# Hymba layer, Up stage: when the weight operands of the next block are made, where the taps stand, and when the weights are fetched

## The chip, the cores and the metric

The kernel runs on one core of one Trainium2 chip. The metric is the device time of one execution in microseconds (us). The median of three runs before the change is 1077.51 us (1074.84 to 1078.73).

## What is computed

One decoder layer on x (1024 x 1024, float32): attention and retention in a mixer, then a feed-forward part. The change lies in the feed-forward part, of which the reference says:

```python
h = rms_norm(x, ffn_pre_norm[l])
u = causal_depthwise_conv(jnp.einsum('bsd,df->bsf', h, w_up[l]), conv_w[l], conv_b[l])
u_gate, u_val = jnp.split(u, 2, axis=-1)
y = jax.nn.gelu(u_gate, approximate=True) * u_val
y = jnp.einsum('bsf,fd->bsd', y, w_down[l])
x = x + rms_norm(y, ffn_post_norm[l])
```

with D_MODEL 1024, D_FF 2816 (22 blocks of 128 for the gate and 22 for the value) and a convolution of three taps.

## The kernel before, in words

The Up product is done in 22 blocks. A block i holds 128 columns of the gate and 128 of the value, and its four quarters (gate and value by the two halves of the sequence) come out of a Strassen-Winograd scheme of seven products, named by their weight operand: B11, T1, T2, B21, T3, T4 and B22. A product (`prod`) is 4 x 3 matmuls of 128x128 by 128x512: each float32 operand is split into a high and a low float32r part, and `mm3` adds high*high, low*high and high*low. For blocks 0 to 10 (early blocks, `EARLY = 11`) the products B11 and B21 have been made in an earlier stage and lie in DRAM (`ud`), so they need five products here; blocks 11 to 21 (late blocks) need all seven. The order is 11, 0, 12, 1, ..., 21, 10, so a pair of blocks is 12 products, 144 matmuls.

In PSUM a block has the accumulator PA (in a row: B11 or, in an early block, the stored part and T2; then T2, T3 and T4 are added), PC (T1, then B22 added) and, if late, PB (B21). PA is copied out between the products that are added to it: `h` after the first (L796), `u` after T2 (L808, late blocks only) and after T3 (L814), `uv` after T4 (L819), all on ACT. DVE adds: `ug` low half from PB and h (L811), `uv` high half from PC and u (L815), `ug` high half from PC (L821). The first product of the next block (`head`) is issued between T3 and T4 of the running one.

The weights of a block come by two transfers of 512 KB (L721: a11 and a12 in the first, a21 and a22 in the second) into a tile `raw`. Of the pool's eight slots six hold activations in this stage, so two `raw` tiles live at once, and the next fetch waits until the last split of the older one has been read out. DVE makes combinations of the quarters (L732, L733, L735, L743), and each operand is split: the high part on ACT (L114 in `oh`, or L712 in `sh`), the low part on DVE (L115, L713). `sh` has four slots and `oh` five, so a split also waits for the product that used its slot.

The gate of a block (`gate`, `taps`) is the convolution: for value and gate ACT makes the first tap (L701), DVE adds two more (L704); then GELU on ACT (L829), the product on DVE (L830) and a store to DRAM (`yd`, 512 KB). SP issues all these transfers in order on one queue. The Down stage (matmuls pd, steps of 24 matmuls) loads yd and w_d, combines and splits them in the same way (`feed`, L848, L115, L713).

The program is written block by block: `prep(then)` fetches and makes all operands of the next block, `strassen(i, then)` issues the products, `gate` the convolution. That is not the order in which the engines get them: a scheduler sorts the instructions by its own model of their times and of free slots, except where `in_turn` ties them to the written order. On each engine the sorted instructions are then run strictly one after the other.

Of the kernel before, what the change touches and what calls it, by code (L numbers as in the profile page):

```python
# [11 lines left out]
ALU = mybir.AluOpType  # L12
# [15 lines left out]
def tile_hymba_layer(  # L28
# [29 lines left out]
    def small(name):  # L58
        return pss.tile([P, H], F32, tag="psm", name=name)
# [99 lines left out]
    def ttile(name, dt=F32):  # L159
        return m.tile([P, H], dt, tag="t", name=name, bufs=5)  # L160
# [507 lines left out]
    for hh in range(2):  # L668
# [5 lines left out]
        if hh == 0:  # L674
# [25 lines left out]
    def taps(a, u, b, c0, n=H):  # L700
        nc.scalar.activation(a, u[:, c0 : c0 + n], AF.Identity, scale=cvp[:, b, 2:3], bias=cvp[:, b, 3:4])  # L701
        for d, tap in ((1, 1), (2, 0)):
            s = max(0, d - c0)
            nc.vector.scalar_tensor_tensor(  # L704
                out=a[:, s:], in0=u[:, c0 + s - d : c0 + n - d], scalar=cvp[:, b, tap : tap + 1], in1=a[:, s:],
                op0=ALU.mult, op1=ALU.add,
            )

    def ssplit(src, name):
        hi = ftile(0, f"sh_{name}", F32R)  # L710
        lo = ftile(1, f"sl_{name}", F32R)
        in_turn("sh", nc.scalar.activation(hi, src, AF.Copy))  # L712
        nc.vector.tensor_tensor(out=lo, in0=src, in1=hi.bitcast(F32), op=ALU.subtract)  # L713
        return hi, lo

    ops = {}

    def prep(i):
        raw = ttile(f"raw{i}", F32)
        for t in range(2):  # L720
            nc.sync.dma_start(raw[:, 2 * t : 2 * t + 2, :], w_u[t * NF + i].rearrange("p (a b) -> p a b", a=2))  # L721
        a11, a12, a21, a22 = [raw[:, c, :] for c in range(4)]
        o = {}
        ug[i] = gtile(f"ug{i}")
        if i < EARLY:
            seeds[i] = ftile(2, f"p1_{i}")
            nc.sync.dma_start(seeds[i], ud[i, :, 0:H])
            nc.sync.dma_start(ug[i][:, 0:H], ud[i, :, H:D])
        else:
            o["B11"] = split(a11, f"u{i}a11")  # L730
        s3, s1 = a11, a21
        nc.vector.tensor_tensor(out=s3, in0=a11, in1=a21, op=ALU.subtract)  # L732
        nc.vector.tensor_tensor(out=s1, in0=a21, in1=a22, op=ALU.add)  # L733
        s2 = xtile(f"s2_{i}")
        nc.vector.tensor_tensor(out=s2, in0=a22, in1=s3, op=ALU.subtract)  # L735
        if i < EARLY:
            o["T2"] = ssplit(s2, f"u{i}s2")
            o["T1"] = ssplit(s1, f"u{i}s1")
        else:
            o["T1"] = ssplit(s1, f"u{i}s1")  # L740
            o["T2"] = ssplit(s2, f"u{i}s2")
            o["B21"] = split(a12, f"u{i}a12")
        nc.vector.tensor_tensor(out=s2, in0=a12, in1=s2, op=ALU.subtract)  # L743
        o["T3"] = ssplit(s3, f"u{i}s3")
        o["T4"] = split(a22, f"u{i}a22")
        o["B22"] = ssplit(s2, f"u{i}s4")
        ops[i] = o
# [17 lines left out]
    ug, seeds, heads = {}, {}, {}  # L765

    def early_load(i):
        raw = load_w(w_u[i], 1024, f"e{i}")
# [19 lines left out]
    def head(i):  # L788
        ps = big(f"PA_{i}")
        u = ftile(2, f"h{i}")  # L790
        if i < EARLY:
            nc.scalar.activation(ps, seeds.pop(i), AF.Copy)
            prod(i, "T2", ps, first=False)
        else:
            prod(i, "B11", ps)
        nc.scalar.activation(u, ps, AF.Copy)  # L796
        heads[i] = ps, u

    def strassen(i, then):
        pa, u = heads.pop(i)  # L800
        g, v = ug.pop(i), vtile(f"uv{i}")
        pc = small(f"PC_{i}")
        prod(i, "T1", pc)
        u2 = u
        if i >= EARLY:
            prod(i, "T2", pa, first=False)
            u2 = ftile(2, f"u2_{i}")
            nc.scalar.activation(u2, pa, AF.Copy)  # L808
            pb = (small, big)[i % 2](f"PB_{i}")
            prod(i, "B21", pb)  # L810
            nc.vector.tensor_tensor(out=g[:, lo], in0=pb, in1=u, op=ALU.add)  # L811
# [12 lines left out]
    def gate(i, g, v):
        a = []
        for t, u in enumerate((v, g)):
            a.append(wtile(f"a{t}_{i}"))
            taps(a[t], u, (1 - t) * NF + i, 0, D)
        nc.scalar.activation(a[1], a[1], AF.Gelu_apprx_tanh)  # L829
        nc.vector.tensor_tensor(out=a[1], in0=a[0], in1=a[1], op=ALU.mult)  # L830
        nc.sync.dma_start(yd[i], a[1])
# [219 lines left out]
    prep(order[0])  # L1051
    head(order[0])
    for i, then in zip(order, order[1:] + [None]):
        if then is not None:
            prep(then)
        else:
# [99 lines left out]
```

## Time and profile before

| | |
|---|---|
| median of three runs | 1077.51 us (1074.84 to 1078.73) |
| the profiled execution's own time | 1077.63 us |
| its span, first to last instruction | 1075.6 us |
| share of the span busy: PE / DVE / ACT / POOL | 98% / 77% / 55% / 10% |
| the Up stage: first weight load of a head to the first wait of Down | 481.6 to 855.5 us |
| mean granted TensorE clock | 0.997 |

A PE row "busy" hides waits, since matmuls overlap: one takes 389 ns but they start every 0.23 us. The waits are therefore read from the weight loads (PEld), one of which stands ahead of each matmul. In timelines the bracket at the end of a row gives the idle time of that engine just before and what ended it.

### The profile page before, as it was taken

To read this page: it belongs to the slowest core of one execution; us is meant where nothing else is said; L and a number is where in the kernel's file an instruction comes from. 1 tells how busy PE (TensorE), PEld (TensorE's weight loads), DVE (VectorE), ACT (ScalarE), POOL (GpSimd) and SP (SyncE) were. 2 spreads that over 40 slices of the span, in tenths; PEclk is the share of its full clock that TensorE was granted. 3 is DMA by queue.
4 is the path that set the end of the run, shared out by engine and by line. 5 is a ranking of instruction groups with operands and counts; after the bars stand their busy time and mean duration, and the time that the engine had idled before them with its cause. 6 is when DMAs were issued, how large, how long until landed. Compare 5 with 4: busy or idle time off the path is not lost.

```text
span 1075.6 us, 14268 instructions
## 1 busy us (share of the span) xinstructions
PE 1051.2 (98%) x5004; PEld 886.6 (82%) x5004; DVE 829.6 (77%) x1428; ACT 587.2 (55%) x1140; POOL 103.9 (10%) x123
## 2 busy tenths in 40 slices
PE   8999999999999999999999999999999999999995
PEld 6988998988988888888887787787878788888884
DVE  5567768668676686987796887968789998859687
ACT  6556763467643567664555455544555545444461
POOL 1013232124322210000000000000000000000011
PEclk9999999999999999999999999999999999999998
DMA  8421551221231473763323323232233784625663
GB/s 287 138 79 59 177 167 51 80 83 55 78 101 57 169 242 125 267 229 124 137 98 118 118 79 137 92 124 91 106 131 115 263 301 140 225 98 189 231 194 129
DMA packets 54727, 152.81 MB, mean 142 GB/s; under 512 B 6400, under 2 KB 6528, under 8 KB 54656
## 3 DMA queue, kind: packets, MB, share of 16 engines
q1 hardware_dynamic: 53504, 149.81, 40.7%
q10 hardware_dynamic: 1152, 2.10, 0.5%
q8 instruction: 39, 0.64, 0.2%
q14 instruction: 32, 0.26, 0.1%
HBM read 126.20 MB, written 25.69 MB: 141 GB/s over the span
## 4 chain that ended last, share of the span: by engine, by line
PE 63%; DVE 17%; DMA 9%; issue 6%; ACT 4%; POOL 1%; SPq 0%; DVEq 0%; POOLq 0%; ACTq 0%
DMA raw<-w_u 6%; DVE a L704 6%; PE pd L123 5%; PE pd L124 5%; PE pd L125 5%; PE ps_r L123 3%; PE ps_r L125 3%; PE ps_r L124 3%; PE po L123 3%; PE po L125 3%; PE po L124 3%; PE pn L123 2%; PE pn L124 2%; PE pn L125 2%; PE PA L123 2%
## 5 line engine op out<-in xcount | busy, mean ns | idle before, releaser
L123 PE MATMUL pd<-oh_d,sh_d 128*128 128x512 f32 x264 | 102.8, 389 | 1.0 <-DVE ug L821 1.0
L124 PE MATMUL pd<-ol_d,sh_d 128*128 128x512 f32 x264 | 102.7, 389 | 0.0
L125 PE MATMUL pd<-oh_d,sl_d 128*128 128x512 f32 x264 | 102.7, 389 | 0.0
L973 POOL TENSOR_TENSOR fs<-fs,mhalf 128x1 f32<-128x1 f32 x8 | 5.8, 730 | 623.6 <-DVE fs L972 623.6
L123 PE MATMUL pn<-oh_n,xh 128*128 128x384 f32 x192 | 65.8, 343 | 0.2 <-DVE gp L285 0.2
L125 PE MATMUL pn<-oh_n,xl 128*128 128x384 f32 x192 | 64.5, 336 | 0.0
L124 PE MATMUL pn<-ol_n,xh 128*128 128x384 f32 x192 | 64.3, 335 | 0.0
L704 DVE SCALAR_TENSOR_TENSOR a<-uv,cvp,a 128x1023 f32<-128x1023 f32 (+1 forms) x44 | 56.2, 1277 | 9.5 <-ACT a L701 9.5
L123 PEld LDWEIGHTS pd<-oh_d,sh_d 128*128 128x128 f32 x264 | 49.5, 188 | 11.7 <-DVE ug L821 1.4
L125 PEld LDWEIGHTS pd<-oh_d,sl_d 128*128 128x128 f32 x264 | 49.5, 188 | 10.3
L124 PEld LDWEIGHTS pd<-ol_d,sh_d 128*128 128x128 f32 x264 | 49.6, 188 | 10.2
L704 DVE SCALAR_TENSOR_TENSOR a<-ug,cvp,a 128x1023 f32<-128x1023 f32 (+1 forms) x44 | 56.2, 1277 | 0.5 <-ACT a L701 0.5
L123 PE MATMUL ps_r<-xh,oh_r 128*128 128x512 f32 x128 | 50.7, 396 | 0.0
L125 PE MATMUL ps_r<-xh,ol_r 128*128 128x512 f32 x128 | 50.0, 390 | 0.0
L124 PE MATMUL ps_r<-xl,oh_r 128*128 128x512 f32 x128 | 49.9, 390 | 0.0
L701 ACT ACTIVATE a<-ug,cvp 128x1024 f32<-128x1024 f32 x22 | 27.4, 1246 | 38.0 <-DVE ug L821 35.7
L331 ACT ACTIVATE s<-s,sc,r 128x128 f32<-128x128 f32 x64 | 31.0, 487 | 29.6 <-DVE sc L325 29.6
L732 DVE TENSOR_TENSOR raw<-raw 128x512 f32<-128x512 f32 x22 | 15.2, 689 | 37.5 <-DMA raw<-w_u 37.5
L829 ACT ACTIVATE a<-a 128x1024 f32<-128x1024 f32 x22 | 23.4, 1062 | 36.2 <-DVE a L704 36.2
L712 ACT ACTIVATE sh_d<-r 128x512 fp32r<-128x512 f32 x33 | 20.9, 632 | 39.5 <-PE pd L124 22.2
L114 ACT ACTIVATE oh_o<-wr_o 128x512 fp32r<-128x512 f32 x32 | 19.9, 634 | 36.8 <-PE po L125 35.6
L114 ACT ACTIVATE oh_n<-wr_n 128x384 fp32r<-128x384 f32 x48 | 24.3, 523 | 28.7 <-PE ps_q L124 10.3
(1177 smaller groups left out, 3293.8 us busy)
## 6 DMA issues: line engine op xcount, KB each, us to landing
raw<-w_u SPq DMA_DIRECT2D x44, 512.0 KB, 4.5
yd<-a SPq DMA_DIRECT2D x22, 512.0 KB, 3.3
r<-yd SPq DMA_DIRECT2D x22, 512.0 KB, 5.8
wr_n<-w_inN SPq DMA_DIRECT2D x24, 384.0 KB, 3.0
wr_r<-w_inT SPq DMA_DIRECT2D x16, 512.0 KB, 3.3
wr_o<-w_o SPq DMA_DIRECT2D x16, 512.0 KB, 3.5
wr_e<-w_u SPq DMA_DIRECT2D x11, 512.0 KB, 4.7
ud<-e SPq DMA_DIRECT2D x11, 512.0 KB, 3.9
```

Of the source, the lines that this page charges most:

```text
L114: in_turn("oh", nc.scalar.activation(hi[:, :n], src, AF.Copy))
L123: ins = nc.tensor.matmul(ps, lh, rh, start=first, stop=False, skip_group_check=onto)
L124: nc.tensor.matmul(ps, lh, rl, start=False, stop=False, skip_group_check=onto)
L125: nc.tensor.matmul(ps, ll, rh, start=False, stop=end, skip_group_check=onto)
L331: nc.scalar.activation(s[:, i, :], s[:, i, :], AF.Exp, scale=r8, bias=c[:, 1, i : i + 1], accum_out=c[:, 3, i : i + 1])
L701: nc.scalar.activation(a, u[:, c0 : c0 + n], AF.Identity, scale=cvp[:, b, 2:3], bias=cvp[:, b, 3:4])
L704: nc.vector.scalar_tensor_tensor(out=a[:, s:], in0=u[:, c0 + s - d : c0 + n - d], scalar=cvp[:, b, tap : tap + 1], in1=a[:, s:], op0=ALU.m ...
L712: in_turn("sh", nc.scalar.activation(hi, src, AF.Copy))
L732: nc.vector.tensor_tensor(out=s3, in0=a11, in1=a21, op=ALU.subtract)
L829: nc.scalar.activation(a[1], a[1], AF.Gelu_apprx_tanh)
L973: nc.gpsimd.tensor_tensor(out=ss[:, 2:3], in0=ss[:, 3:4], in1=mhalf[:, 0:1], op=ALU.pow)
```

## The change

`prep` is cut into `fetch` (the two transfers, and the stored part of an early block), `fetch_g` (the tile ug and its stored half), `combos` (B11's split if late, then three combinations) and `part` (the split of one named operand). `body` replaces `strassen` and `gate`: it issues the products of block i and, at written places between them, `make` for the operands of the next block. The convolution of the block before is written in two halves inside the running block (`gate_v` value, `gate_g` gate, GELU, product and store). `fetch` is called for the block after the next at the start of a block. In early blocks T1 is issued after T3. The last gate is written behind the splits of the first two Down steps.

```diff
-    def prep(i):
-        raw = ttile(f"raw{i}", F32)
+    def fetch(i):
+        raw = raws[i] = ttile(f"raw{i}", F32)
         for t in range(2):
             nc.sync.dma_start(raw[:, 2 * t : 2 * t + 2, :], w_u[t * NF + i].rearrange("p (a b) -> p a b", a=2))
+        if i < EARLY:
+            seeds[i] = ftile(3, f"p1_{i}")
+            nc.sync.dma_start(seeds[i], ud[i, :, 0:H])
+        ops[i] = {}
+
+    def fetch_g(i):
         ug[i] = gtile(f"ug{i}")
         if i < EARLY:
-            seeds[i] = ftile(2, f"p1_{i}")
-            nc.sync.dma_start(seeds[i], ud[i, :, 0:H])
             nc.sync.dma_start(ug[i][:, 0:H], ud[i, :, H:D])
...
+    def combos(i):
+        if i >= EARLY:
+            part(i, "B11")
+        raw = raws[i]
+        a11, a12, a21, a22 = [raw[:, c, :] for c in range(4)]
+        s2 = s4s[i] = xtile(f"s2_{i}")
+        nc.vector.tensor_tensor(out=a11, in0=a11, in1=a21, op=ALU.subtract)
+        nc.vector.tensor_tensor(out=s2, in0=a22, in1=a11, op=ALU.subtract)
+        nc.vector.tensor_tensor(out=a21, in0=a21, in1=a22, op=ALU.add)
+
+    def part(i, *names):
+        raw = raws[i]
+        for x in names:
+            if x == "B22":
+                nc.vector.tensor_tensor(out=s4s[i], in0=raw[:, 1, :], in1=s4s[i], op=ALU.subtract)
...
-    def strassen(i, then):
+    def body(i, then, before):
+        def make(*names):
+            if then is not None:
+                part(then, *names)
+
         pa, u = heads.pop(i)
-        g, v = ug.pop(i), vtile(f"uv{i}")
-        pc = small(f"PC_{i}")
-        prod(i, "T1", pc)
-        u2 = u
-        if i >= EARLY:
+        g, pc = ug.pop(i), small(f"PC_{i}")
+        full = i >= EARLY
+        if then is not None:
+            combos(then)
+        if full:
+            prod(i, "T1", pc)
+            make("T2")
+            if before:
+                gate_v(*before)
             prod(i, "T2", pa, first=False)
             u2 = ftile(2, f"u2_{i}")
             nc.scalar.activation(u2, pa, AF.Copy)
+            make("T3")
             pb = (small, big)[i % 2](f"PB_{i}")
             prod(i, "B21", pb)
+            if before:
+                gate_g()
+            if then is not None:
+                fetch_g(then)
             nc.vector.tensor_tensor(out=g[:, lo], in0=pb, in1=u, op=ALU.add)
+        else:
+            gate_v(*before)
+        v = vtile(f"uv{i}")
         prod(i, "T3", pa, first=False)
-        u3 = ftile(2, f"u3_{i}")
+        u3 = ftile(3, f"u3_{i}")
         nc.scalar.activation(u3, pa, AF.Copy)
+        if not full:
+            u2 = u
+            prod(i, "T1", pc)
         nc.vector.tensor_tensor(out=v[:, hi], in0=pc, in1=u3, op=ALU.add)
+        make("T1")
+        if not full:
+            gate_g()
+            if then is not None:
+                fetch_g(then)
         if then is not None:
             head(then)
+        if not full:
+            make("T2", "T3", "B21")
+        make("T4")
         prod(i, "T4", pa, first=False)
         nc.scalar.activation(v[:, lo], pa, AF.Copy)
+        if then is None:
+            feed(0)
         prod(i, "B22", pc, first=False)
         nc.vector.tensor_tensor(out=g[:, hi], in0=pc, in1=u2, op=ALU.add)
-        return g, v
...
+        make("B22")
+        return i, g, v
...
+    for k, i in enumerate(order):
+        if k + 2 < len(order):
+            fetch(order[k + 2])
+        if k + 1 == len(order):
             for t in range(AHEAD_LOAD):
                 load(t)
-            feed(0)
-        gate(i, *strassen(i, then))
-    ready = 1
+        before = body(i, order[k + 1] if k + 1 < len(order) else None, before)
+    feed(1)
+    gate_v(*before)
+    gate_g()
+    ready = 2
```

The scheduler decides what this makes of each engine's order. Three places in the middle of the stage show it (late blocks 18 and 19, early blocks 6, 7 and 8).

ACT, from the copy of block 18's head to its copy after T2 (oh_u19 are the splits of block 19's B11 and B21, `a` the convolution's tiles of block 6, sh_u18 the last split of block 18, sh_u7 splits of block 7). Before:

```order
L796 ACTIVATE h_6857<-PA_6856 128x512
L114 ACTIVATE oh_u19a_7054<-raw_7050 128x512
L819 ACTIVATE uv_6827<-PA_6737 128x512
L792 ACTIVATE PA_6997<-p_7_6912 128x512
L701 ACTIVATE a_6_6897<-uv_6827,cvp 128x1024
L114 ACTIVATE oh_u19a_7070<-raw_7050 128x512
L712 ACTIVATE sh_u18s_6823<-s_18_6800 128x512
L701 ACTIVATE a_6_6901<-ug_6651,cvp 128x1024
L712 ACTIVATE sh_u7s_6919<-s_7_6917 128x512
L712 ACTIVATE sh_u7s_6923<-raw_6908 128x512
L808 ACTIVATE u_18_6966<-PA_6856 128x512
```

and now:

```order
L797 ACTIVATE h_6841<-PA_6840 128x512
L862 ACTIVATE uv_6800<-PA_6731 128x512
L701 ACTIVATE a_6_6926<-uv_6800,cvp 128x1024
L712 ACTIVATE sh_u18B_6898<-s_18_6792 128x512
L114 ACTIVATE oh_u19B_7048<-raw_6902 128x512
L114 ACTIVATE oh_u19B_7123<-raw_6902 128x512
L701 ACTIVATE a_6_6961<-ug_6708,cvp 128x1024
L712 ACTIVATE sh_u7T_6922<-s_7_6906 128x512
L712 ACTIVATE sh_u7T_6944<-raw_6782 128x512
L832 ACTIVATE u_18_6942<-PA_6840 128x512
```

The first split of block 19 stood second, ahead of the copy `uv` and both first taps of block 6; it now stands behind `uv`, the value's tap and the last split of block 18, and the splits of B11 and B21 are neighbours.

DVE, in the early block 7, from the first combination of block 8's weights (raw_7168 before, raw_7042 now) to the `uv` add. Before (12 rows from the combination on):

```order
L732 TENSOR_TENSOR raw_7168<-raw_7168 128x512
L733 TENSOR_TENSOR raw_7168<-raw_7168 128x512
L704 SCALAR_TENSOR_TENSOR a_18_7039<-uv_6940,cvp,a_18_7039 128x1023
L821 TENSOR_TENSOR ug_6793<-PC_6941,u_18_6966 128x512
L704 SCALAR_TENSOR_TENSOR a_18_7039<-uv_6940,cvp,a_18_7039 128x1022
L713 TENSOR_TENSOR sl_u19s_7063<-raw_7050,sh_u19s_7062 128x512
L704 SCALAR_TENSOR_TENSOR a_18_7043<-ug_6793,cvp,a_18_7043 128x1023
L713 TENSOR_TENSOR sl_u19s_7067<-s_19_7060,sh_u19s_7066 128x512
L704 SCALAR_TENSOR_TENSOR a_18_7043<-ug_6793,cvp,a_18_7043 128x1022
L743 TENSOR_TENSOR s_19_7060<-raw_7050,s_19_7060 128x512
L713 TENSOR_TENSOR sl_u19s_7076<-raw_7050,sh_u19s_7075 128x512
L815 TENSOR_TENSOR uv_7087<-PC_7088,u_7_7113 128x512
```

and now (from the second combination on; the first stands just ahead of it, as before):

```order
L739 TENSOR_TENSOR s_8_7166<-raw_7042 128x512
L704 SCALAR_TENSOR_TENSOR a_18_7056<-uv_6971,cvp,a_18_7056 128x1023
L866 TENSOR_TENSOR ug_6839<-PC_6905,u_18_6942 128x512
L704 SCALAR_TENSOR_TENSOR a_18_7056<-uv_6971,cvp,a_18_7056 128x1022
L713 TENSOR_TENSOR sl_u19T_7089<-raw_6902,sh_u19T_7088 128x512
L704 SCALAR_TENSOR_TENSOR a_18_7092<-ug_6839,cvp,a_18_7092 128x1023
L713 TENSOR_TENSOR sl_u19T_7116<-s_19_7052,sh_u19T_7115 128x512
L704 SCALAR_TENSOR_TENSOR a_18_7092<-ug_6839,cvp,a_18_7092 128x1022
L850 TENSOR_TENSOR uv_7060<-PC_7047,u_7_7073 128x512
L713 TENSOR_TENSOR sl_u19T_7120<-raw_6902,sh_u19T_7119 128x512
L812 TENSOR_TENSOR a_18_7092<-a_18_7056,a_18_7092 128x1024
L746 TENSOR_TENSOR s_19_7052<-raw_6902,s_19_7052 128x512
```

The first combination of block 8 has kept its place; the `uv` add has moved ahead of two operations, and the last operation that reads the weights of block 19 (s_19, L746) has moved from ahead of the split of T3 to behind the product `a` (L812).

SP, the same stretch: stores `yd`, weight fetches `raw`, stored parts p and ug. Before:

```order
L831 DMA yd<-a_6_6901 128x1024
L721 DMA raw_7168<-w_u 128x1024 x2
L728 DMA ug_7171<-ud 128x512
L721 DMA raw_7310<-w_u 128x1024
L727 DMA p_8_7172<-ud 128x512
L831 DMA yd<-a_18_7043 128x1024
L721 DMA raw_7310<-w_u 128x1024
L831 DMA yd<-a_7_7161 128x1024
```

and now:

```order
L813 DMA yd<-a_6_6961 128x1024
L724 DMA p_8_7045<-ud 128x512
L721 DMA raw_7042<-w_u 128x1024 x2
L730 DMA ug_7228<-ud 128x512
L813 DMA yd<-a_18_7092 128x1024
L721 DMA raw_7162<-w_u 128x1024 x2
L813 DMA yd<-a_7_7221 128x1024
```

The two halves of a late block's weights (raw_7310, now raw_7162) were issued one before and one behind the store of block 18; now both stand behind it.

## Rows read from the trace of the kernel before

**Rows 1.** The page, part 1: busy us (share of the span) xinstructions.

```profile
PE 1051.2 (98%) x5004; PEld 886.6 (82%) x5004; DVE 829.6 (77%) x1428; ACT 587.2 (55%) x1140; POOL 103.9 (10%) x123
```

**Rows 2.** Windows by engine: busy (x instructions); then granted clock, DMA share, GB/s.

```profile
470.00:482.00 12.00, 12.00 (x54) 9.85 (x53) 8.90 (x16) 5.50 (x11) 0.00 (x0) 1.00 0.94 336
...
584.00:822.00 238.00, 231.66 (x1009) 188.27 (x1009) 193.07 (x248) 125.48 (x185) 0.00 (x0) 1.00 0.31 109
822.00:856.00 34.00, 31.93 (x138) 25.22 (x137) 30.13 (x40) 17.81 (x26) 0.00 (x0) 1.00 0.71 242
856.00:880.00 24.00, 24.00 (x108) 19.85 (x107) 23.49 (x36) 12.08 (x20) 0.00 (x0) 1.00 0.63 234
```

**Rows 3.** Waits of the weight loads, 480 to 862: us in total, times, longest.

```profile
PEld PA L123 <- ACT u L808: 8.7, 7, 2.7
PEld PC L123 <- DVE uv L815: 2.7, 5, 1.0
PEld PA L123 <- ACT u L814: 1.8, 2, 1.4
PEld pd L123 <- DVE ug L821: 1.4, 1, 1.4
```

**Rows 4.** The tile PA: weight loads of two heads; the range is of their starts.

```profile
L123 PEld LDWEIGHTS PA<-hh,oh_u11a x4: 187/188/188, 481.6 to 483.6; 128*128 128x128 f32 x4
...
L123 PEld LDWEIGHTS PA<-T2h,sh_u0s x4: 188/188/188, 495.2 to 497.2; 128*128 128x128 f32 x4
```

**Rows 5.** Timeline of the weight loads: start, us, operation, idle before it.

```profile
591.51 0.19 PEld L123 LDWEIGHTS PA<-T3h,sh_u14s 128*128 128x128 f32 x1 [1.14 <-ACT u L808]
...
855.54 0.19 PEld L123 LDWEIGHTS pd<-oh_d,sh_d 128*128 128x128 f32 x1 [1.38 <-DVE ug L821]
```

**Rows 6.** Timeline of DVE, one early block, 604 to 614.5.

```profile
604.27 0.69 DVE L732 TENSOR_TENSOR raw<-raw 128x512 f32<-128x512 f32 x1 [3.61 <-DMA raw<-w_u]
...
605.61 1.28 DVE L704 SCALAR_TENSOR_TENSOR a<-uv,cvp,a 128x1023 f32<-128x1023 f32 x1
606.80 0.68 DVE L821 TENSOR_TENSOR ug<-PC,u 128x512 f32<-128x512 f32 x1
607.40 1.27 DVE L704 SCALAR_TENSOR_TENSOR a<-uv,cvp,a 128x1022 f32<-128x1022 f32 x1
...
613.99 1.21 DVE L830 TENSOR_TENSOR a<-a,a 128x1024 f32<-128x1024 f32 x1
```

**Rows 7.** Timeline of SP: when the weight fetches were issued.

```profile
578.47 0.33 SPq L721 DMA_DIRECT2D raw<-w_u  x1
...
598.89 1.00 SPq L721 DMA_DIRECT2D raw<-w_u  x2
...
613.50 0.33 SPq L721 DMA_DIRECT2D raw<-w_u  x1
...
615.23 0.33 SPq L831 DMA_DIRECT2D yd<-a  x1
...
632.93 0.81 SPq L721 DMA_DIRECT2D raw<-w_u  x2
...
782.91 0.33 SPq L721 DMA_DIRECT2D raw<-w_u  x1
```

**Rows 8.** Timeline of ACT: splits that wait for weights, and what follows.

```profile
583.37 0.63 ACT L114 ACTIVATE oh_u15a<-raw 128x512 fp32r<-128x512 f32 x1 [4.49 <-DMA raw<-w_u]
...
588.69 1.25 ACT L701 ACTIVATE a<-ug,cvp 128x1024 f32<-128x1024 f32 x1 [1.51 <-DVE ug L821]
...
617.42 0.63 ACT L114 ACTIVATE oh_u16a<-raw 128x512 fp32r<-128x512 f32 x1 [3.51 <-DMA raw<-w_u]
...
787.51 0.63 ACT L114 ACTIVATE oh_u21a<-raw 128x512 fp32r<-128x512 f32 x1 [4.20 <-DMA raw<-w_u]
```

**Rows 9.** The line of the weight fetch: time from issue to landing.

```profile
DMA to landing us min/median/max: 3.4/4.5/7.8
```

**Rows 10.** Timeline of DVE at the start of the Down stage.

```profile
860.79 0.68 DVE L115 TENSOR_TENSOR ol_d<-rt,oh_d 128x512 fp32r<-128x512 f32 x1
```

More of the change, by code (lines that the diff above doesn't have):

```diff
@@ L716, in tile_hymba_layer @@
     ops = {}
-    def prep(i):
-        raw = ttile(f"raw{i}", F32)
+    def fetch(i):
+        raw = raws[i] = ttile(f"raw{i}", F32)
         for t in range(2):
             nc.sync.dma_start(raw[:, 2 * t : 2 * t + 2, :], w_u[t * NF + i].rearrange("p (a b) -> p a b", a=2))
-        a11, a12, a21, a22 = [raw[:, c, :] for c in range(4)]
-        o = {}
+        if i < EARLY:
[3 more added lines that the diff above has]
+    def fetch_g(i):
@@ L724, in prep @@
         ug[i] = gtile(f"ug{i}")
         if i < EARLY:
-            seeds[i] = ftile(2, f"p1_{i}")
-            nc.sync.dma_start(seeds[i], ud[i, :, 0:H])
             nc.sync.dma_start(ug[i][:, 0:H], ud[i, :, H:D])
[L729 to L747, printed above, removed]
+    def combos(i):
[7 more added lines that the diff above has]
+        nc.vector.tensor_tensor(out=a21, in0=a21, in1=a22, op=ALU.add)
@@ L749, in operand @@
+    def part(i, *names):
[3 more added lines that the diff above has]
+                nc.vector.tensor_tensor(out=s4s[i], in0=raw[:, 1, :], in1=s4s[i], op=ALU.subtract)
+            src = {"B11": raw[:, 0, :], "T1": raw[:, 2, :], "T3": raw[:, 0, :], "B21": raw[:, 1, :], "T4": raw[:, 3, :]}.get(x)
+            ops[i][x] = (split if x in ("B11", "B21", "T4") else ssplit)(s4s[i] if src is None else src, f"u{i}{x}")
     def operand(xn):
@@ L764, in tile_hymba_layer @@
     lo, hi = slice(0, H), slice(H, D)
-    ug, seeds, heads = {}, {}, {}
+    ug, seeds, heads, raws, s4s = {}, {}, {}, {}, {}
     def early_load(i):
@@ L797, in head, with gate_v, gate_g @@
         heads[i] = ps, u
-    def strassen(i, then):
-        pa, u = heads.pop(i)
-        g, v = ug.pop(i), vtile(f"uv{i}")
-        pc = small(f"PC_{i}")
-        prod(i, "T1", pc)
-        u2 = u
-        if i >= EARLY:
+    gates = []
+    def gate_v(i, g, v):
+        a = wtile(f"a0_{i}")
+        taps(a, v, NF + i, 0, D)
+        gates.append((i, g, a))
+    def gate_g():
+        i, g, a0 = gates.pop()
+        a1 = wtile(f"a1_{i}")
+        taps(a1, g, i, 0, D)
+        nc.scalar.activation(a1, a1, AF.Gelu_apprx_tanh)
+        nc.vector.tensor_tensor(out=a1, in0=a0, in1=a1, op=ALU.mult)
+        nc.sync.dma_start(yd[i], a1)
+    def body(i, then, before):
+        def make(*names):
+            if then is not None:
+                part(then, *names)
+        pa, u = heads.pop(i)
+        g, pc = ug.pop(i), small(f"PC_{i}")
[7 more added lines that the diff above has]
+                gate_v(*before)
             prod(i, "T2", pa, first=False)
@@ L808, in strassen @@
             nc.scalar.activation(u2, pa, AF.Copy)
+            make("T3")
             pb = (small, big)[i % 2](f"PB_{i}")
             prod(i, "B21", pb)
+            if before:
+                gate_g()
+            if then is not None:
+                fetch_g(then)
             nc.vector.tensor_tensor(out=g[:, lo], in0=pb, in1=u, op=ALU.add)
+        else:
+            gate_v(*before)
+        v = vtile(f"uv{i}")
         prod(i, "T3", pa, first=False)
-        u3 = ftile(2, f"u3_{i}")
+        u3 = ftile(3, f"u3_{i}")
         nc.scalar.activation(u3, pa, AF.Copy)
+        if not full:
+            u2 = u
+            prod(i, "T1", pc)
         nc.vector.tensor_tensor(out=v[:, hi], in0=pc, in1=u3, op=ALU.add)
+        make("T1")
[3 more added lines that the diff above has]
+                fetch_g(then)
         if then is not None:
             head(then)
+        if not full:
+            make("T2", "T3", "B21")
+        make("T4")
         prod(i, "T4", pa, first=False)
         nc.scalar.activation(v[:, lo], pa, AF.Copy)
+        if then is None:
+            feed(0)
         prod(i, "B22", pc, first=False)
         nc.vector.tensor_tensor(out=g[:, hi], in0=pc, in1=u2, op=ALU.add)
-        return g, v
[L824 to L831, printed above, removed]
+        make("B22")
+        return i, g, v
     act2[0] = (st_out[0]["hi"], st_out[0]["lo"])
@@ L1050, in tile_hymba_layer @@
     order = [i for c in range(EARLY) for i in (EARLY + c, c)]
-    prep(order[0])
-    head(order[0])
[L1053 to L1056, printed above, removed]
+    fetch(order[0])
+    combos(order[0])
+    part(order[0], "T1", "T2", "T3", "B21", "T4", "B22")
+    fetch(order[1])
+    fetch_g(order[0])
+    head(order[0])
+    before = None
+    for k, i in enumerate(order):
+        if k + 2 < len(order):
+            fetch(order[k + 2])
+        if k + 1 == len(order):
             for t in range(AHEAD_LOAD):
                 load(t)
-            feed(0)
-        gate(i, *strassen(i, then))
-    ready = 1
+        before = body(i, order[k + 1] if k + 1 < len(order) else None, before)
[3 more added lines that the diff above has]
+    ready = 2
     held = []
```

## The prediction

> **What bounds the kernel now.** The page's busy times come first: PE is busy 98% of the span, DVE 77% [rows 1]. Over the whole run only PE's waits can be won, so I look for them in the stage that the change touches. The windows show that PE does wait there: in 584 to 822 it is busy 231.66 of 238 us, in 822 to 856 31.93 of 34 [rows 2]. Overlapping matmuls hide part of a wait, so its true size is read from the weight loads: between 480 and 862 they waited 8.7 us for the copy after T2 (L808), 2.7 for the `uv` add (L815), 1.8 for the copy after T3 (L814) and 1.4 for the `ug` add (L821), together 14.6 us [rows 3]. That is the most that better placing can give: 1077.63 - 14.6 = 1063.0 us.
>
> Next, why PE waits. Five products take 13.6 us, from 481.6 to 495.2 [rows 4], so one takes 2.72 and a pair of blocks (12 products) 32.6 us. The pairs in fact repeat every 34.0 us: the split of block 15 starts at 583.37, that of block 21, six pairs later, at 787.51 [rows 8]. Something other than PE has a period of 34.0, and the timelines of SP, DVE and ACT show it as a ring with two transfers in it. An early block's weights are issued at 598.89 [rows 7], DVE waits 3.61 us for them and starts the first combination at 604.27 [rows 6]: 5.4 us. It works through that block until the late weights can be issued at 613.50 [rows 7]: 9.2 us. ACT waits 3.51 us and starts the split of B11 at 617.42 [rows 8]: 3.9 us. The next early fetch goes out at 632.93 [rows 7]: 15.5 us. Sum 34.0. Each fetch waits for the last reader of the older tile, so the ring turns at its own pace, 1.4 us slower than PE. PE starts the stage with a lead: its first wait is at 591.51, in the fourth pair [rows 5]. Three pairs cost 4.2 us of lead, seven more cost 9.8; the rows have 8.7 + 2.7 = 11.4 for them. I use **loss = 10 x (ring - 32.6) - 4.2**, and nothing if that is negative.
>
> **The change, part by part.** Nothing is computed more or less: the sorted orders have the same number of rows on PE, ACT, DVE and SP. All that counts is who stands behind what.
>
> Fetching two blocks ahead: costed at nothing, gains nothing. With two weight tiles the fetch still waits for the last split of the older tile, and the first combination of the next early block has kept its place four operations later. Both landings in the ring stay as they are, and so does DVE's 3.6 us wait.
>
> First DVE leg. The late fetch now waits for L746 behind the product, not for the split of T3. Ahead of it the leg has two operations more: the `uv` add and the product. An add takes 0.60 (606.80 to 607.40), a tap 1.19 (605.61 to 606.80), the product about 1.15 (1.21 less the overlap of two operations) [rows 6]. 9.2 + 0.60 + 1.15 = 11.0 us.
>
> Second leg. Before, the split of B11 stood ahead of `uv`, the first taps and everything behind them: from its start at 583.37 to the gate's first tap at 588.69 passed 5.3 us [rows 8]. Now `uv`, the value's tap and the `ug` add run while the weights are still on their way, and behind the landing there are only: two splits on ACT, 0.53 each, the gate's tap 1.25, then thirteen operations on DVE in the new order (two taps, the product, ten of 0.60) up to the last split of the early tile: 2.4 + 1.15 + 6.0 + 0.1 = 9.65. Sum 1.05 + 1.29 + 9.65 = 12.0 us for 15.5.
>
> New ring: 5.4 + 11.0 + 3.9 + 12.0 = **32.3 us, under PE's 32.6**. PE is then the slower one, and L808's 8.7 us go. Bounds 0 and 8.7 left; I take 0, but the margin is only 0.3 us a pair, with 0.4 more from the lead spread over ten pairs. One thing is not in that sum: both late halves are now issued behind the store `yd`, which before stood between them. The store is 0.6 us ahead. At the highest rate in the rows, 336 GB/s [rows 2], 512 KB take 1.56 us, so the first half lands 0 to 0.95 us later than before. Up to 0.7 costs nothing, 0.95 gives 10 x 0.65 - 4.2 = 2.3 us; I take 0 and keep 2.3 for the range.
>
> The `uv` add is 1.2 us earlier, ahead of a combination and a split, and its longest wait was 1.0 [rows 3]: 2.7 go, 0 left (bounds 0 and 2.7). T1 behind T3 in early blocks: in the last block, where no head stands between, T4 followed T3 at once and had to wait for the copy of PA, 1.4 of L814's 1.8 us [rows 3]; now T1's 2.72 us cover it. 0.4 left (bounds 0 and 1.8). The `ug` add that frees the fourth Down tile, waited for at 855.54 [rows 5], has about one operation less ahead of it: I leave 0.7 of 1.4 (bounds 0 and 1.4).
>
> What is late next: the start of Down. DVE is full there, 23.49 of 24 us in 856 to 880 [rows 2], with the last two convolutions and the first feeds. The wait at 855.54 came 9 matmuls into the first Down step, so that step began near 853.5 and the third, 48 matmuls of 0.227 later, at 864.4. Its last split ended at 861.5 [rows 10], and is needed only in the second half of the step: 2.9 + 2.7 = 5.6 us ahead. If PE comes 12 us sooner and DVE gains nothing, 12 - 5.6 = 6.4 us are lost; if DVE moves along, none. DVE should mostly move along, since its waits are for weights and products that come sooner too; following the new order by the same durations I find the third step's last split 2.4 us ahead of its use. I book 1.5, nearer to none.
>
> Sum: 0.4 + 0.7 + 1.5 = 2.6 us of waits left of 14.6, so 12.0 saved: 1077.63 - 12.0 = 1065.6 us for the profiled execution, whose time is 0.1 above the median of the three runs: **1065.5 us**.
>
> **The rivals.** *Start of Down takes it back.* DVE stays as late as before and 6.4 us are lost in place of 1.5: 1070.5. For: DVE has no gaps there. Against: its feeds wait for slots that products free.
>
> *The store in front.* A late fetch begins only when the whole store has drained: 1.56 us later instead of at most 0.95. Ring 33.9, loss 10 x 1.3 - 4.2 = 8.8, with the 2.6 above 11.4 left: 1074.4. For: one queue, and the store always just ahead. Against: a first half took 4.9, 3.9 and 4.6 us from issue to use (578.47 to 583.37, 613.50 to 617.42, 782.91 to 787.51) [rows 7, 8] with other transfers about. The Trainium skill ("DMA: Bandwidth & Descriptors", section "Queues, rings and completion order") has it that SP's transfers share one ring on each DMA engine and are consumed in ring order, which speaks for this rival; no row of this trace shows a fetch so placed.
>
> *It does not do what it says.* The fetches are no earlier and most orders keep their shape. If the ring stays at 34.0, only the waits at the end go: about 1076. For: the unmoved first combination. Against: B11's split, which has clearly moved.
>
> *Slower.* ACT's two splits of late weights now stand ahead of the gate's tap, two splits of the running early block and the copy after T2, and wait for a half that is issued 1.75 us later in DVE's order. Each us that it lands later turns the ring 1 us slower. To lose 0.5% the waits must reach 14.6 + 5.4 = 20, so 17.4 in the ring, a ring of 34.8, and a landing 2.5 us above 3.9, at 6.4 us. Landings go up to 7.8, with a median of 4.5 [rows 9]. At 7.8 throughout: ring 36.2, loss 31.8, and 1077.6 - 14.6 + 34.4 = 1097. For: the store in front. Against: DMA engines are busy 31% in 584 to 822 [rows 2].
>
> **How the numbers follow.** A measurement of this kernel can tell about 0.5%, 5.4 us, from no change. Forecast 0.60 (1063 to 1069), start of Down 0.12 (1070.5), store in front 0.12 (1074.4), no effect 0.10 (1076), slower 0.06. Faster by over 0.5%, below 1072.1: 0.60 + 0.12 and a sixth of the store's rival, 0.74. Slower 0.06, the rest 0.20. The range starts at 1063.0 less some 1.5 of scatter between runs and goes up past the store's rival: 1061.5 to 1075, leaving out the slower case and most of "no effect".
>
> **What would show it.** Right: pairs repeat every 32.6 to 32.8 us; no wait for the copy after T2; ACT's split of B11 waits under 1 us; DVE still waits some 3 us for early weights; DVE now waits for ACT's tap on `uv`, so for PE. Wrong: a period near 34 with waits for that copy; a late first half that lands 6 us after its issue; or waits of pd on its splits between 840 and 880, where there is none now.

## The result and the profile after

| | before | after |
|---|---|---|
| median | 1076.47 us (six runs, 1074.84 to 1078.73) | 1065.89 us (six runs, 1064.66 to 1066.98) |
| profiled execution: own time / span | 1077.63 / 1075.6 us | 1064.66 / 1063.0 us |
| granted TensorE clock | 0.997 | 0.997 |

The ratio of the runs is 0.9892, 95% interval 0.9872 to 0.9913: faster by 1.1%. The forecast was 1065.5 us.

The stage that the change touches is full now. In the windows of the changed kernel (columns as in [rows 2]) PE is busy in every microsecond from 584 to 845 and on:

```profile
584.00:822.00 238.00, 238.00 (x1052) 197.14 (x1051) 200.99 (x258) 130.81 (x188) 0.00 (x0) 1.00 0.33 112
822.00:845.00 23.00, 23.00 (x102) 18.59 (x101) 19.02 (x26) 13.67 (x20) 0.00 (x0) 1.00 0.84 287
845.00:869.00 24.00, 24.00 (x108) 19.87 (x107) 24.00 (x37) 11.38 (x19) 0.00 (x0) 1.00 0.63 223
```

Of the 14.6 us of waits of the weight loads [rows 3] two rows are left between 480 and 880, 0.6 us:

```profile
PEld PC L123 <- DVE uv L850: 0.4, 1, 0.4
PEld pd L123 <- DVE ug L866: 0.2, 1, 0.2
```

The waits for the copy after T2 (now L832) and for the copy after T3 (L846) are gone. The first load of the stage is where it was, and the load that waits for the fourth Down tile comes at 843.20 instead of 855.54 [rows 5] (timeline of the weight loads):

```profile
481.66 0.19 PEld L123 LDWEIGHTS PA<-hh,oh_u11B 128*128 128x128 f32 x1
...
843.20 0.19 PEld L123 LDWEIGHTS pd<-oh_d,sh_d 128*128 128x128 f32 x1 [0.18 <-DVE ug L866]
843.31 0.19 PEld L124 LDWEIGHTS pd<-ol_d,sh_d 128*128 128x128 f32 x1
843.54 0.19 PEld L125 LDWEIGHTS pd<-oh_d,sl_d 128*128 128x128 f32 x1
```

From 481.66 to 843.20 are 361.5 us, before 373.9: 12.4 of the 12.6 us by which the span is shorter lie in this stage. The waits, though, shrank by 14.0. The three last rows say why: behind a wait the next load follows after 0.11 us, the one after it at the usual 0.23. All fifteen waits of [rows 3] have the same short step behind them (0.10 to 0.11 us). So every wait gives back some 0.12 us, the fifteen 1.8 us, and with thirteen waits fewer 14.0 of waits are 12.4 of time.

Now the ring: the chain of two fetches that wait for each other's tiles. SP's timeline has its fetches and the stores ahead of them:

```profile
611.88 0.33 SPq L813 DMA_DIRECT2D yd<-a  x1
612.53 0.92 SPq L721 DMA_DIRECT2D raw<-w_u  x2
...
629.07 0.81 SPq L721 DMA_DIRECT2D raw<-w_u  x2
644.59 0.33 SPq L813 DMA_DIRECT2D yd<-a  x1
645.24 0.92 SPq L721 DMA_DIRECT2D raw<-w_u  x2
...
661.64 0.81 SPq L721 DMA_DIRECT2D raw<-w_u  x2
```

and DVE's and ACT's have the first operations on what was fetched, with their waits in brackets, of DVE:

```profile
634.15 0.69 DVE L738 TENSOR_TENSOR raw<-raw 128x512 f32<-128x512 f32 x1 [3.31 <-DMA raw<-w_u]
```

and of ACT, with the copy `uv` that stands ahead of it now and waits for PE:

```profile
612.64 0.60 ACT L862 ACTIVATE uv<-PA 128x512 f32<-128x512 f32 x1 [1.56 <-PE PA L125]
...
617.09 1.15 ACT L114 ACTIVATE oh_u16B<-raw 128x512 fp32r<-128x512 f32 x2 [1.32 <-DMA raw<-w_u]
...
645.28 0.60 ACT L862 ACTIVATE uv<-PA 128x512 f32<-128x512 f32 x1 [1.49 <-PE PA L125]
...
649.66 1.15 ACT L114 ACTIVATE oh_u17B<-raw 128x512 fp32r<-128x512 f32 x2 [1.25 <-DMA raw<-w_u]
```

The copies `uv` at 612.64 and 645.28 are one pair apart: 32.64 us, PE's own 12 x 2.72. The four legs of the ring, in the turn that these rows show (before as in the prediction):

| leg | before | predicted | after |
|---|---|---|---|
| early fetch issued to DVE's first combination | 5.4 | 5.4 | 5.08 (629.07 to 634.15) |
| to the late fetch | 9.2 | 11.0 | 11.09 (to 645.24) |
| to ACT's split of B11 | 3.9 | 3.9 | 4.42 (to 649.66) |
| to the next early fetch | 15.5 | 12.0 | 11.98 (to 661.64) |
| sum | 34.0 | 32.3 | 32.57 |

The two legs of the engines come out alike in every turn from 601 on (11.08 to 11.09, and 11.98), while the landings differ: 4.8 to 6.3 us for the early weights, 4.3 to 5.0 for B11's. So one turn can mislead. The nine turns from the fetch at 496.84 to that at 791.87 took 32.78 us in the mean, before 34.03 (496.79 to 803.03); the longest, 33.91 us from 595.16, has the landing of 6.3. The ring is thus as long as PE's 32.64 and not below it, and the 1.3 us that it was longer over nine turns are covered by PE's lead. The questions were whether there is room in it, and which part of the change made it short.

### The profile page after: what moved, and what is told of

Read it like the earlier page. It is cut to its first block, busy times and chain, and to the rows that moved or that the text cites. A ratio compares the mean times of both kernels' runs of the same rounds, so it can differ in the third digit from the quotient of the medians.

```text
span 1063.0 us, 14272 instructions
## 1 busy us (share of the span) xinstructions
PE 1047.1 (99%) x5004; PEld 887.4 (83%) x5004; DVE 828.9 (78%) x1428; ACT 591.8 (56%) x1140; POOL 103.4 (10%) x123
## 4 chain that ended last, share of the span: by engine, by line
PE 88%; DVE 7%; issue 1%; DMA 1%; POOL 1%; ACT 1%; SPq 0%; DVEq 0%; POOLq 0%; ACTq 0%
PE PA L125 7%; PE PA L123 7%; PE PA L124 7%; PE pd L123 5%; PE pd L124 5%; PE pd L125 5%; PE PC L123 4%; PE PC L125 4%; PE PC L124 4%; PE pn L123 3%; PE pn L124 3%; PE pn L125 3%; PE ps_r L123 3%; PE ps_r L125 3%; PE ps_r L124 3%; PE po L123 3%
## 5 line engine op out<-in xcount | busy, mean ns | idle before, releaser
L704 DVE SCALAR_TENSOR_TENSOR a<-uv,cvp,a 128x1023 f32<-128x1023 f32 (+1 forms) x44 | 56.2, 1278 | 14.3 <-ACT a L701 14.3
L738 DVE TENSOR_TENSOR raw<-raw 128x512 f32<-128x512 f32 x22 | 15.1, 688 | 33.2 <-DMA raw<-w_u 33.2
L115 DVE TENSOR_TENSOR ol_o<-wr_o,oh_o 128x512 fp32r<-128x512 f32 x32 | 22.7, 716 | 18.4 <-ACT oh_o L114 18.2
```

Source lines behind the costliest of these rows:

```text
L704: nc.vector.scalar_tensor_tensor(out=a[:, s:], in0=u[:, c0 + s - d : c0 + n - d], scalar=cvp[:, b, tap : tap + 1], in1=a[:, s:], op0=ALU.m ...
L738: nc.vector.tensor_tensor(out=a11, in0=a11, in1=a21, op=ALU.subtract)
```

## Experiments

All medians stand beside runs of the kernel before on the same chip, 1076.1 to 1079.0 us. Ratios are to these, and kernels measured on different chips are best compared by them; the changed kernel has 0.9892 (1065.89 us, waits 0.6 us).

| kernel | median us | ratio, 95% interval | PE waits 480 to 880, us |
|---|---|---|---|
| before, B11's split late | 1068.76 | 0.9900 (0.9885 to 0.9914) | 2.4 |
| before, T1 behind T3 | 1077.00 | 0.9992 (0.9977 to 1.0006) | 15.1 |
| before, late weights in `wr` | 1066.67 | 0.9882 (0.9867 to 0.9896) | 2.6 |
| before, nine splits moved | 1067.41 | 0.9907 (0.9877 to 0.9937) | 3.1 |
| after, B11's split early | 1067.14 | 0.9894 (0.9876 to 0.9911) | 2.2 |
| after, T1 in front | 1067.85 | 0.9910 (0.9882 to 0.9938) | 2.1 |
| after, fetch one ahead | 1065.93 | 0.9892 (0.9862 to 0.9922) | 0.7 |
| after, last gate first | 1065.09 | 0.9886 (0.9853 to 0.9918) | 0.9 |
| after, late weights in `wr` | 1065.81 | 0.9893 (0.9865 to 0.9922) | 1.0 |
| after, tile released late | 1087.10 | 1.0069 (1.0042 to 1.0095) | 23.7 |
| after, store twice | 1076.55 | 0.9979 (0.9965 to 0.9993) | 14.3 |

### One part alone: B11's split late, T1 behind T3

In `prep` of a late block `vtaps[-2]` is the value tap of the early block whose `uv` stood behind the split; `behind` sets an order, no wait.

```diff
-        in_turn("oh", nc.scalar.activation(hi[:, :n], src, AF.Copy))
+        ins = nc.scalar.activation(hi[:, :n], src, AF.Copy)
+        in_turn("oh", ins)
+        if after:
+            behind(ins, after)
...
-            o["B11"] = split(a11, f"u{i}a11")
+            o["B11"] = split(a11, f"u{i}a11", after=vtaps[-2] if len(vtaps) > 1 else None)
```

> The kernel before with one order changed: on ACT the split of B11 of the next late block (L114) stands behind the early block's copy uv and its value tap. Fetches, products and the places of the taps stay as written. Theory (the ring): that split was what held the gate behind the weights, so the leg from it to the next early fetch shrinks from 15.5 to about 12 us, the ring from 34.0 to some 30.5, under PE's 32.6; the pairs then repeat every 32.6 to 32.8 us, the 8.7 us of waits for the copy after T2 go and the 1.4 us of the last block stay: 1067 to 1071 us. Rival (the split's place is not the cause, it was the fetch two blocks ahead, the taps set apart or T1 behind T3): period 34.0, 1075 to 1079.

1068.76 us, as the ring has it. The weights have landed before ACT gets to them, so its row has no wait, and PE's waits are the last block's and the `ug` add's (waits of the weight loads, then ACT):

```profile
PEld PA L126 <- ACT u L829: 1.4, 1, 1.4
PEld pd L126 <- DVE ug L836: 1.0, 1, 1.0
```

```profile
612.99 1.24 ACT L704 ACTIVATE a<-uv,cvp 128x1024 f32<-128x1024 f32 x1
614.14 1.14 ACT L114 ACTIVATE oh_u16a<-raw 128x512 fp32r<-128x512 f32 x2
```

DVE waits for the value's tap, so for PE, 1.2 to 2.4 us in every pair (here with the first combination, which starts the first leg):

```profile
599.94 0.69 DVE L747 TENSOR_TENSOR raw<-raw 128x512 f32<-128x512 f32 x1 [2.73 <-DMA raw<-w_u]
...
614.26 1.28 DVE L709 SCALAR_TENSOR_TENSOR a<-uv,cvp,a 128x1023 f32<-128x1023 f32 x1 [2.11 <-ACT a L704]
```

The next late fetch is issued at 609.17, so the first leg is 9.2 us as before, not the 11.1 of the changed kernel. This part alone is enough.

The second run has T1 behind T3 and nothing else:

```diff
-        prod(i, "T1", pc)
         u2 = u
         if i >= EARLY:
+            prod(i, "T1", pc)
...
         nc.scalar.activation(u3, pa, AF.Copy)
+        if i < EARLY:
+            prod(i, "T1", pc)
```

> The kernel before with T1 behind T3 in the early blocks and nothing else. Theory: this takes away the last block's wait of T4 for the copy after T3 (1.4 us) and leaves the ring alone: pairs every 34.0 us, waits for the copy after T2 still about 8.7 us, 1074 to 1077 us. Rival (the place of T1 gives DVE and ACT the time that breaks the ring): period 32.6 to 33, 1066 to 1070 us.

1077.00 us, no difference, and the ring is left alone: ACT's split of B11 waits as before, at 585.30, 619.00 and 652.62, 33.7 us apart. One thing came out otherwise: the waits are no longer for the copy after T2 but for the `uv` add:

```profile
PEld PC L123 <- DVE uv L817: 12.3, 9, 1.9
PEld PA L123 <- ACT u L808: 2.1, 6, 0.5
PEld pd L123 <- DVE ug L823: 0.7, 1, 0.7
```

15.1 us in all for 14.6. Where PE is stopped depends on which product comes first behind DVE's late work; how long, on the ring. The last block's 1.4 us are gone, but the ring gives PE no use for them.

### The ring taken apart: late weights in another pool

```diff
+        else:
+            raw = [load_w(w_u[t * NF + i], 1024, f"l{t}_{i}") for t in range(2)]
+            a11, a12, a21, a22 = [w[:, c : c + H] for w in raw for c in (0, H)]
```

> The kernel before, late blocks' weights fetched into two tiles of the pool wr (idle in this stage) in place of a slot of the pool T. An early fetch then no longer waits for a late block's last split, nor a late one for an early block's: the ring has no link any more, while the split of B11 still stands ahead of the copy uv on ACT. Theory (the ring of two fetches that wait for each other's tiles): period 32.6 to 32.8 us, waits of DVE for early weights under 1 us, the waits for the copy after T2 go: 1065 to 1070 us. Rival (it was the order on ACT itself, whatever the fetches do): period 34, 1075 to 1079 us.

1066.67 us. DVE's wait for weights in the tiles `raw`, 35.9 us in eleven times before (ten of them early blocks), is 0.2 in all, and PE's waits for the copy after T2 are gone, although B11's split still stands ahead of `uv`:

```profile
DVE raw L736 <- DMA raw<-w_u: 0.2, 1, 0.2
```

So it was the two fetches waiting for each other's tiles, not ACT's order in itself. The same in the changed kernel:

> The changed kernel with the late weights in two tiles of the pool wr, so that the early and the late fetches no longer wait for each other's tiles. Theory: PE is already the slower one in this stage, with 0.6 us of waits left between 480 and 862, so taking DVE's 3 us waits away gains nothing: 1064.5 to 1067.5 us, pairs every 32.64 us. Rival (a later wait of the weights still costs something in the stage): 1062 to 1064 us.

1065.81 us: nothing is gained, with DVE's waits for weights down from 33.0 to 0.6 us. In the changed kernel PE is the bound, and those 3 us waits cost nothing.

### The change with one part undone

First the split of B11, put back ahead of `uv`:

```diff
         if i >= EARLY:
             part(i, "B11")
+            if len(uvs) > 1:
+                behind(uvs[-2], last["oh"])
```

(`uvs` holds the copies `uv`; the early block's is set behind the split.)

> The changed kernel with the split of B11 put back ahead of the early block's copy uv on ACT; fetches, taps and T1 as in the changed kernel. Theory (the ring): the second leg grows by about 3.5 us. The sum of the prediction gives a ring of 35.8 us and 10 x 3.2 - 4.2 = 28 us of loss, 1094 us; with some 1 us a pair of slack (DVE waits that long for the value tap in the changed kernel) 34.8 us and 18 us of loss, 1084. So 1080 to 1094, with waits for the copy after T2. Rival (the place of this split does not matter once the fetches are two ahead): 1065 to 1068 us and pairs every 32.64 us.

A miss: 1067.14 us, not 1080 to 1094. The split does stand ahead of `uv` and waits for its weights (ACT):

```profile
617.42 0.63 ACT L114 ACTIVATE oh_u16B<-raw 128x512 fp32r<-128x512 f32 x1 [5.89 <-DMA raw<-w_u]
617.95 0.58 ACT L874 ACTIVATE uv<-PA 128x512 f32<-128x512 f32 x1
```

but the leg behind it is 12.6 us (13.2 in every other pair), not 15.5 (SP):

```profile
630.01 0.84 SPq L731 DMA_DIRECT2D raw<-w_u  x2
```

DVE shows where the 2.9 us stay away. In both kernels it makes B11's low part at 618.08; the split that frees the early tile ends the leg, at 632.22 before and at 629.29 here. Before:

```profile
618.08 0.69 DVE L115 TENSOR_TENSOR ol_u16a<-raw,oh_u16a 128x512 fp32r<-128x512 f32 x1 [1.67 <-ACT oh_u16a L114]
...
632.22 0.68 DVE L713 TENSOR_TENSOR sl_u4s<-raw,sh_u4s 128x512 fp32r<-128x512 f32 x1
```

and with the split put back:

```profile
618.08 0.69 DVE L115 TENSOR_TENSOR ol_u16B<-raw,oh_u16B 128x512 fp32r<-128x512 f32 x1 [1.21 <-ACT oh_u16B L114]
...
629.29 0.68 DVE L713 TENSOR_TENSOR sl_u4T<-raw,sh_u4T 128x512 fp32r<-128x512 f32 x1
```

Before, the stretch has 18 operations, here 14: the `ug` add stands ahead of it, and two low parts and a combination of the late block behind it. So in the changed kernel the split's place costs only 0.6 to 1.3 us of this leg, because four DVE operations fewer stand ahead of the release. That these operations are a price whatever they are for is a theory of its own, and it was tried on the kernel before, with ACT's order as it was (the order of DVE, ACT and SP tied to its own, nine instructions of DVE moved). DVE's order in one block:

```diff
 ug<-PB,h
+sl_u4s<-raw,sh_u4s
 raw<-raw
 s_16<-raw
 ol_u16a<-raw,oh_u16a
-sl_u4s<-raw,sh_u4s
 uv<-PC,u_15
```

> The kernel before with the order of DVE, ACT and SP in the Up stage tied to its own, but for nine instructions of DVE: the last split that reads an early block's weight tile (sl of T3, for blocks 1 to 9) stands three operations earlier, ahead of the two combinations and one low part of the next late block. B11's split stays ahead of the copy uv on ACT, T1 and the taps stay. Theory (the ring is a sum of what stands ahead of each release, whatever those operations are for): the tile comes free 3 x 0.60 = 1.8 us earlier, the ring is 34.0 - 1.8 = 32.2 us, under PE's 32.6: pairs every 32.6 to 32.8 us, the 8.7 us of waits for the copy after T2 go, 2 to 5 us of the others stay: 1067 to 1071 us. Rival (what counts is that B11's split on ACT holds uv and the gate): period 34, 1075 to 1080 us.

1067.41 us. ACT's split of B11 still waits and still holds `uv`, the freeing split comes at 626.21 and the fetch right behind it:

```profile
612.87 0.63 ACT L121 ACTIVATE oh_u16a<-raw 128x512 fp32r<-128x512 f32 x1 [2.82 <-DMA raw<-w_u]
613.41 0.58 ACT L826 ACTIVATE uv<-PA 128x512 f32<-128x512 f32 x1
```

```profile
626.93 0.81 SPq L728 DMA_DIRECT2D raw<-w_u  x2
...
659.57 0.82 SPq L728 DMA_DIRECT2D raw<-w_u  x2
```

The fetches are 32.64 us apart, PE's pair, and these waits are left:

```profile
PEld PA L130 <- ACT u L821: 1.4, 1, 1.4
PEld pd L130 <- DVE ug L828: 1.3, 1, 1.3
PEld PC L130 <- DVE uv L822: 0.4, 1, 0.4
```

Nine moved splits give nearly all that the change gives; of the rest, the first row is what T1 behind T3 takes away.

Next, the changed kernel with T1 in front of T3 again in the early blocks:

```diff
         else:
+            u2 = u
+            prod(i, "T1", pc)
             gate_v(*before)
...
-        if not full:
-            u2 = u
-            prod(i, "T1", pc)
```

> The changed kernel with T1 in front of T3 again in the early blocks. Theory: the last block's T4 has no product between it and T3's copy any more: its wait of 1.4 us comes back, and some of the 2.7 us for the uv add may; the ring stays under 32.6 us: 1067 to 1070 us, pairs every 32.6 to 32.8 us. Rival (T1's place is part of what broke the ring): period 33 to 34, 1072 to 1080 us.

1067.85 us, 2.0 above the changed kernel, which the intervals do not set apart; the rows do. The last block's wait for the copy after T3 is back:

```profile
PEld PA L123 <- ACT u L848: 1.4, 1, 1.4
PEld pd L123 <- DVE ug L865: 0.7, 1, 0.7
```

Each fetch written one block ahead, not two:

```diff
-        if k + 2 < len(order):
-            fetch(order[k + 2])
+        if 1 < k + 1 < len(order):
+            fetch(order[k + 1])
```

> The changed kernel with each fetch written one block ahead, as before, in place of two. On the queues only the stored parts p and one first fetch change places. Theory (a fetch is bound by the release of its tile, not by where it is written): no difference, 1064.5 to 1067.5 us, DVE's waits for early weights still about 3 us each. Rival (the fetch two ahead brings weights earlier): those waits grow and 2 us or more are lost, over 1068 us.

1065.93 us, no difference. The engines get the same orders but for two rows on DVE and some stored parts on SP, and DVE waits as long:

```profile
DVE raw L738 <- DMA raw<-w_u: 32.5, 11, 3.6
```

The last gate ahead of the second Down step's splits:

```diff
-    feed(1)
     gate_v(*before)
     gate_g()
-    ready = 2
+    ready = 1
```

> The changed kernel with the last gate written ahead of the second Down step's splits, as before. Theory: DVE is full at the start of Down, but the third step's last split was some 2 us ahead of its use, and the order moves only single operations: 1065 to 1067 us, no waits of pd on its splits. Rival (the place of the last gate is what kept Down from taking 6.4 us back): waits of pd on its splits of 2 to 6 us, 1068 to 1072 us.

1065.09 us, no difference and no wait of pd on a split.

### How near the edge: a late release, a second store

In both, the orders of DVE, ACT and SP in the Up stage are tied to those of the changed kernel, so that nothing else moves there. The first adds a tiny DVE operation that reads the early tile three operations after its last split, and so frees it later:

```diff
         make("B22")
+        if full and then is not None:
+            nc.vector.tensor_tensor(
+                out=gn[:, 0:1], in0=raws[then][:, 2, 0:1], in1=ops[then]["B22"][1][:, 0:1].bitcast(F32), op=ALU.add
+            )
```

> The changed kernel with the order of DVE, ACT and SP in the Up stage tied to that of the changed kernel, and one tiny DVE operation (128x1) added behind the last split of each early block that also reads that block's weight tile: the tile comes free, and the next early fetch can be issued, three DVE operations later, about 1.9 us. No product's operand is later by more than that tiny operation. Theory (the ring, summed from the changed kernel's trace: 5.08 + 11.09 + 4.42 + 11.98 = 32.57 us, as good as PE's 32.64, so with no slack): the ring becomes 34.5, the loss 10 x 1.9 - 4.2 = 14.4 us: 1076 to 1081 us, pairs every 34.2 to 34.6 us once the lead is used up, and the waits for the copy after T2 or for the uv add are back. Rival (the ring follows PE and has slack of its own, DVE's 3 us waits included): 1065 to 1068 us, pairs every 32.64 us.

1087.10 us, 21 above the changed kernel (19 by the ratios), where 14 were expected: the direction of the theory, with more loss. The stage itself, from the first load to the wait for the fourth Down tile, is 21.1 us longer (481.46 to 864.07). DVE frees the tile three operations later, then waits 5.09 instead of 3.31 us:

```profile
637.06 0.69 DVE L720 TENSOR_TENSOR sl_u4T<-raw,sh_u4T 128x512 fp32r<-128x512 f32 x1
...
639.59 0.16 DVE L876 TENSOR_TENSOR gn<-raw,sl_u4B 128x1 f32<-128x1 f32 x1
644.84 0.69 DVE L745 TENSOR_TENSOR raw<-raw 128x512 f32<-128x512 f32 x1 [5.09 <-DMA raw<-w_u]
```

The early fetches go out at 605.34, 639.81 and 674.26, every 34.46 us: 1.9 longer than 32.57, as summed. Over all nine periods (499.65 to 813.82) the mean is 34.9, since a few landings were slower (5.7 us at 690.30, 6.1 at 535.04), and the first fetch was already 2.8 us later than the 496.84 of the changed kernel. 9 x (34.9 - 32.64) + 2.8 = 23 us: of the lead of 4.2 us that I had counted on, some 2 were there. PE waits for the copy after T3 and the `uv` add:

```profile
PEld PA L130 <- ACT u L853: 11.9, 10, 2.3
PEld PC L130 <- DVE uv L857: 7.7, 17, 0.7
```

There is no slack: 1.9 us more ahead of a release cost about ten times as much.

The second issues the store of each late block twice:

```diff
         nc.sync.dma_start(yd[i], a1)
+        if i >= EARLY:
+            nc.sync.dma_start(yx[i], a1)
```

> The changed kernel with the order of DVE, ACT and SP in the Up stage tied to that of the changed kernel, and the store yd of each late block issued a second time, into a DRAM tile of its own, directly ahead of the late fetch: 512 KB more in front of each late half. Output and all else as before. Theory (transfers share the engines, and one store in front has cost nothing: 4.42 us from issue to use against 4.50 before): the late half lands 0 to 0.8 us later, the ring is 32.6 to 33.4, loss 0 to 4 us: 1065 to 1070 us. Rival (a fetch starts only when what stands ahead of it on the queue has drained): 1.56 us later or more, ring 34.1, loss 10 x 1.5 - 4.2 = 10.8: 1075 to 1080 us, and the time from issue to use of a late half near 6 us.

1076.55 us: the rival's number, not mine. SP and ACT:

```profile
615.32 0.33 SPq L821 DMA_DIRECT2D yd<-a  x1
615.69 0.42 SPq L823 DMA_DIRECT2D yx<-a  x1
616.22 1.84 SPq L728 DMA_DIRECT2D raw<-w_u  x2
```

```profile
622.02 1.15 ACT L121 ACTIVATE oh_u16B<-raw 128x512 fp32r<-128x512 f32 x2 [4.50 <-DMA raw<-w_u]
```

From issue to use 5.8 us here, 5.83 in the mean of eight blocks (5.26 to 6.31), against 4.51 in the mean of six of the changed kernel: 1.3 later, near the 1.56 that a whole store takes at 336 GB/s [rows 2]. The issue of the second store on SP puts the fetch itself off by another 0.26: the first leg is 11.35 us (604.87 to 616.22), not 11.09. With both the ring is 34.18 us (599.82 to 634.00), 34.3 in the mean of nine turns (496.32 to 804.89). The stage is 11.6 us longer (481.14 to 854.32), the median 10.7 (9.4 by the ratios).

## Why the prediction was right, point by point

- **The bound and the floor.** Right: the time was in PE's waits in this stage, and 14.0 of 14.6 us went. But a microsecond of a load's wait is not quite one of time: the fifteen waits were worth 12.8, so the floor was nearer 1064.8 than 1063.0. The run came to 1064.66, as some 0.6 us were also saved outside this stage.
- **The ring.** Right in the two legs that the change touches: 11.0 and 12.0 predicted, 11.09 and 11.98 measured. The margin of 0.3 us a pair was not there: B11's landing took 4.5 us in the mean where 3.9, one turn's, was booked, and 4.4 was the mean of eight before. That hardly a wait came of a ring of 32.78 is due to the lead, which the formula had as well. Four runs that break the ring in different ways (another pool, B11's split late, nine splits moved, the change) all end at PE's 32.64 us, and two that lengthen it, by 1.9 and 1.6 us, cost the stage 21 and 12.
- **Fetching two blocks ahead is worth nothing.** Shown: one ahead gives the same time.
- **What shortened the second leg.** The sum was right, the weight that I gave to B11's split was not. I read it as the thing that held the gate, and expected 15.5 us back with it. With it back the leg is 12.6 to 13.2, because the other operations of the late block stay behind the early block's last split. In the kernel before either is enough. The change also made the first leg 1.9 us longer, which B11's split moved by itself does not, so it kept less room than that one move leaves: in the changed kernel B11's split waits for its weights in the late turns, there it does not. The gate in two halves and the new places of `make` were not run by themselves.
- **The store in front.** Right in size, 0.1 of the 0 to 0.95 us: 4.51 us from issue to use in the mean, before 4.40 (eight blocks, 3.76 to 5.12). The forecast was close to falling all the same, since a second store costs 1.6 us a pair and takes back nearly the whole gain. The Trainium skill ("DMA: Bandwidth & Descriptors", section "Queues, rings and completion order") has the descriptors of a ring consumed in order on each DMA engine; the run with the store twice agrees with it (1.3 us later), the changed kernel with one store does not show it.
- **`uv` add and T1.** 2.7 us to 0.4 where I wrote 0, and the copy after T3 to 0 where I wrote 0.4. T1 behind T3 is worth its 1.4 us only where the ring does not take them: nothing in the kernel before.
- **The start of Down.** The 1.5 us that I booked were not there: no wait of pd on a split, with the last gate in either place. DVE moved along with PE: the last store `yd` is issued at 852.17, before at 862.72.
- **The sum.** 2.6 us of waits left were booked and 0.6 found, 2.0 too many; the 1.6 us that thirteen waits give back were not booked. The two errors nearly cancel, which is luck: 12.0 us were forecast and the stage gave 12.4. The profiled execution's own time fell by 13.0 (1064.66, where 1065.6 was forecast), 0.6 of it outside the stage.
- **The signs named.** Pairs every 32.64 us, no wait for the copy after T2, DVE still waiting 3.3 us for early weights, and ACT's copy `uv` waiting for PE: all there. ACT's split of B11 waits 0.8 to 1.3 us in the six late blocks from 16 on, a little over the 1 us that I set.

## What to carry to other kernels

Where two buffers pass between transfers and an engine, write the ring down as a sum, from issue to landing, from landing to the last reader, and compare it with the bound engine's period: where the ring is the longer one, the sum tells what each operation ahead of a release costs, times the number of turns, and the bound engine's waits show only where that loss comes out. Then the cheap cure is to move the last reader of a buffer ahead of work that could as well come behind it. A kernel whose ring is only just as short as the period has no room: count what stands ahead of every release before adding to it.

## What was not expected of the hardware

One store of 512 KB on the queue, 0.65 us ahead of a fetch, made it hardly later (4.51 us in the mean of six, against 4.40 in the mean of eight before), a second one directly ahead made it 1.3 us later. SP's own part shows in the same rows: the two halves of the fetch took 0.92 us to issue behind one store and 1.84 behind two. Whether the first store is free because it has its 0.65 us of lead, or because the first half had other transfers beside it before as well, these runs do not tell apart.
